# Memory chunks moved into the first two units' steps, and rotation tables computed in one pass per group

## Chip, cores and metric

The kernel runs on 1 core of one Trainium2 chip. The metric is device microseconds (us) for one execution of the whole program, the median of several runs.

## What is computed

Two encoder layers (DEPTH = 2) over one sequence of 2048 frames of 1024 channels. In each layer one projection of the input feeds four groups of heads, A (banded attention with a relative bias), B (latent attention), C (sliding window with rotary positions) and M (cross-attention into 256 memory tokens). The outputs are gated, concatenated, projected and normalized. The parts that the change touches:

```python
def _rope(x, positions):
    d = x.shape[-1]
    inv_freq = ROPE_THETA ** (-jnp.arange(0, d, 2, dtype=jnp.float32) / d)
    ang = positions.astype(jnp.float32)[..., None] * inv_freq
    cos = jnp.cos(ang)[:, :, None, :]
    sin = jnp.sin(ang)[:, :, None, :]
    x1, x2 = jnp.split(x.astype(jnp.float32), 2, axis=-1)
    return jnp.concatenate([x1 * cos - x2 * sin, x2 * cos + x1 * sin], axis=-1)

def _memory_attention(q, mem, w_mem_kv):
    kv = (mem @ w_mem_kv).reshape(b, MEM_LEN, 2, MEM_HEADS, HEAD_DIM)
    k, v = kv[:, :, 0], kv[:, :, 1]
    sc = jnp.einsum('bqhd,bmhd->bhqm', qh, k).astype(jnp.float32) * (HEAD_DIM ** -0.5)
    p = jax.nn.softmax(sc, axis=-1)
    ...
```

Group C rotates heads of 64 channels (32 frequencies, "group 0" of the tables), group B rotary parts of 32 channels (16 frequencies, "group 1").

## The kernel before

**Tiling.** The sequence is cut into four blocks of 512 frames (BT = 512, `b` = 0 to 3). A projection (`project`, L353) computes one chunk of 128 output channels for one block: eight steps over the 1024 input channels, each of three matmuls, since input and weights are kept as a high and a low part (hi x hi, hi x lo, lo x hi). A chunk's weights (512 KB) are loaded into one of two buffers `raws` (`wload`, L323) and split by ScalarE (high part) and GpSimd (low part; the first eight chunks half by VectorE) into one of two buffers `W` (`wsplit`, L328). The order of all chunks is the list `wsrc`, written out at L311 to L320 from `ORDER`: memory's eight chunks come first, then 23 per block.

**Stages.** At the start, `mem_kv` (L1193) loads memory and splits it, computes the first rotation tables, loads block 0 of x, and projects memory's chunks, first those of layer 1 (written to DRAM, read back by `load_mem`, L1230) and then those of layer 0. Between their steps it splits x. Then, for each layer, phase 1 runs six units per block: C, M and A for the first half of the heads (`p` = 0), then C, M and A for the second half. Phase 2 runs the latent attention, eight units B per layer. Phase 3 (`phase3`, L1325) is the output projection and the norm.

**Order of work.** A unit gives steps ("fill": projections, maxima, with a cost each) and banks (score and value matmuls). `drive` (L1096) runs the first unit's fill by itself and spreads each later unit's fill over the banks of the unit before it. A clock of modelled time (`Clock`, L94) puts off small pieces (`later`, `after`). Below that the framework's scheduler reorders instructions of one engine when their operands are ready, and each engine then runs its own list in order. All DMA issues here stand on SP's queue.

**Rotation tables.** `trig(b, gs)` (L279) computes cosine and signed sine of one block for a group: positions are broadcast to 128 partitions, each partition has its frequency, and the table of 128 rows x 512 holds every frequency four or eight times. It goes to DRAM (`cos`, `sin`). Before a unit that rotates, both are loaded into `cts` with one DMA each: in unit C (L731, L732), for the latents (L827, L828) and in unit B (L968, L969). The tables of group 0 of block 0 are computed in `mem_kv`, those of group 1 of block 0 at the head of unit M's fill, and those of block `b + 1`, both groups, near the head of the sixth unit's fill of block `b`, in layer 0 alone (near L1454). `rope` (L707) multiplies a projection by both tables, moves rows by four DMAs (`us<-u`) and adds.

**Other names.** `max_row` (L482) transposes the row maxima and writes them by DMA (`Y<-mr`, 4 rows of 128) into the query rows; scores wait for them. In unit B the rotated query rows go to their place by DMA (`Y<-xh`, `Y<-xl`, L1035 and L1036), which the maxima (`mx`) wait for. `Y` is one large buffer that the phases share by regions.

Of the kernel before, what the change touches and what calls it, by code (L numbers as in the profile page):

```python
# [11 lines left out]
F32 = mybir.dt.float32  # L12
# [137 lines left out]
def hybrid(ctx, tc, x, mem, positions, w_in, rel_bias, q_norm, w_uq, kv_norm, w_ukv,  # L150
# [117 lines left out]
    cosT, sinT, memkv = {}, {}, {}  # L268
# [10 lines left out]
    def trig(b, gs=(0, 1)):  # L279
        pi = tmp("pi", I32)  # L280
        dma(pi, rowcast(positions, b * BT, BT))
        pf = tmp("pf")
        nc.vector.tensor_copy(pf, pi)
        for g in gs:
            ang, kk = tmp("ang"), tmp("kk")
            nc.vector.tensor_scalar(ang, pf, rc[:, g:g + 1], None, op0=OP.mult)
            nc.vector.tensor_scalar(kk, ang, float(np.float32(1.0 / TWO_PI)), ROUND, op0=OP.mult, op1=OP.add)
            nc.vector.tensor_scalar(kk, kk, -ROUND, None, op0=OP.add)
            for pc in (PC1, PC2, PC3):
                stt(ang, kk, -pc, ang, op0=OP.mult, op1=OP.add)  # L290
            nc.vector.tensor_scalar(ang, ang, 3.1415925, -3.1415925, op0=OP.min, op1=OP.max)
            nc.vector.tensor_scalar(kk, ang, -1.0, None, op0=OP.mult)
            tt(kk, kk, ang, op=OP.max)
            nc.vector.tensor_scalar(kk, kk, -1.0, float(np.float32(math.pi / 2)), op0=OP.mult, op1=OP.add)
            act(ang, ang, AF.Sin)
            act(kk, kk, AF.Sin)
            nc.vector.tensor_scalar(ang, ang, rc[:, 2 + g:3 + g], None, op0=OP.mult)
            cosT[g, b] = dram.tile([128, BT], F32, name=f"cos{g}{b}")
            sinT[g, b] = dram.tile([128, BT], F32, name=f"sin{g}{b}")
            dma(cosT[g, b], kk)  # L300
            dma(sinT[g, b], ang)
# [26 lines left out]
    def wsplit(i):  # L328
        if i < wstate["limit"] and wstate["split"] == i:
# [108 lines left out]
    def put_v(p, vt, t0, n):  # L438
# [3 lines left out]
        def tr():  # L442
# [6 lines left out]
            ck.tick(0.107 * n)  # L449
        after(vf, 0.1, tr)  # L450
# [274 lines left out]
    def unit_c(l, b, p, D):  # L725
# [4 lines left out]
        def tabl():  # L730
            dma(cts[0], cosT[0, b])  # L731
            dma(cts[1], sinT[0, b])  # L732
# [44 lines left out]
        if p == 0:  # L777
# [41 lines left out]
    def latent(l, b, k, p, D):  # L819
# [6 lines left out]
        if k == 0:  # L826
            dma(cts[0], cosT[1, b])  # L827
            dma(cts[1], sinT[1, b])  # L828
# [71 lines left out]
    def unit_m(l, b, p, D):  # L900
# [30 lines left out]
        fill = project((l, b, 14 + 2 * p), qdone)  # L931
        pg = project((l, b, 15 + 2 * p), gdone)
# [16 lines left out]
    def unit_b(l, b, p, D):  # L949
# [13 lines left out]
        def loads():  # L963
# [4 lines left out]
            dma(cts[0], cosT[1, b])  # L968
            dma(cts[1], sinT[1, b])  # L969
# [223 lines left out]
    def mem_kv(kq):  # L1193
        ms = [region(4096 + 2048 * i, 2048).rearrange("p (k c) -> p k c", k=8) for i in range(2)]
        f, st = load_cols([mem[128 * k:128 * k + 128, :] for k in range(8)], 256, xs=ms, ahead=4)
# [12 lines left out]
        wload(3)  # L1208
        early()
        kq()  # L1210
        for ll in range(L - 1, -1, -1):
            for p in range(2):
                def kd(pk, p=p):
                    for i in range(2):
                        split_k(pk[64 * i:64 * i + 64, :256], *Km[2 * p + i])
                run_fill(mix(project(("mem", ll, p), kd, 256, xs=ms), xst[:2]))
                xst = xst[2:]
                run_fill(mix(project(("mem", ll, 2 + p), lambda pv, p=p: put_v(pv, Vm[p], 0, 2), 256, xs=ms), xst[:2]))
                xst = xst[2:]
            if ll:  # L1220
                ck.drain()
                for h in range(4):
                    for i, n in ((0, 128), (1, 64)):
                        memkv[ll, h, i] = dram.tile([n, 256], F32R, name=f"mk{ll}_{h}_{i}")
                        dma(f32(memkv[ll, h, i]), f32(Km[h][i])[0:n])
                for p in range(2):
                    memkv[ll, p] = dram.tile([128, 2, 6, 64], F32R, name=f"mv{ll}_{p}")
                    dma(f32(memkv[ll, p]), f32(Vm[p]))
# [189 lines left out]
    for l in range(L):  # L1418
# [10 lines left out]
        if l == 0:  # L1429
            mem_kv(kq)  # L1430
            ck.drain()
# [3 lines left out]
        units = []  # L1435
        for b in range(NB):
# [82 lines left out]
```

## Time and profile before

| | |
|---|---|
| median of 3 runs | 2660.25 us (2650.18 to 2664.6) |
| profiled execution, its own time | 2660.33 us |
| its span, first to last instruction | 2658.5 us |
| mean clock granted to TensorE | 0.984 of full |
| HBM traffic | 247.43 MB read, 68.02 MB written |

The profile is of one execution. Its page lists each engine's busy time; "L350" is line 350 of the kernel, which for helpers is the helper's line, so groups are told apart by their tiles (`out<-in`). PE is TensorE, DVE is VectorE, ACT is ScalarE, POOL is GpSimd, SP the queue that issues the DMAs. A bracket behind an instruction gives the engine's idle time before it and what released it. Times in a timeline are from the start of the span.

### The profile page before, as it was taken

The page shows a single profiled execution, that of the slowest core. Times are in us where ns is not written, and L with a number is a line of the kernel's source. Part 1 is how long each engine was busy: PE and PEld are TensorE (multiplying, and loading weights), DVE is VectorE, ACT ScalarE, POOL GpSimd, SP SyncE. Part 2 cuts the span into 40 slices and gives each one's busy share as a digit, 9 for nine tenths or more (in the row PEclk, how much of TensorE's full clock was granted, in tenths as well). Part 3 has the DMA queues.
Part 4 walks back from the last instruction along what each step waited for, and adds up shares of the span by engine and source line. Part 5 has one row for each costly group of instructions (what it writes and reads, how often), then busy time and mean ns, then how long its engine had stood idle before and what let it go on. Part 6 is the DMA issues. An engine that isn't in the chain of part 4 may idle for free. (4 is left out here: it accounts for less than half of the span.)

```text
span 2658.5 us, 36518 instructions
## 1 busy us (share of the span) xinstructions
PE 2517.0 (95%) x12312; PEld 2072.1 (78%) x12312; DVE 1864.5 (70%) x3309; ACT 1258.8 (47%) x2251; POOL 1071.2 (40%) x835
## 2 busy tenths in 40 slices
PE   7999999999999899989999999999999999999998
PEld 6777877877888777768877778788788777777786
DVE  4667767658666877878766566567567577588786
ACT  4544455545544566650025444454454555666200
POOL 3343434343443344353343434434434433435343
PEclk9999999999999999999999999999999999999999
DMA  6555345345345423244445443443443453232432
GB/s 208 159 159 168 107 140 158 110 132 166 106 129 169 150 78 98 71 152 145 140 136 160 150 145 127 126 138 118 143 139 115 144 168 104 68 114 78 150 124 87
DMA packets 176443, 350.90 MB, mean 132 GB/s; under 512 B 25689, under 2 KB 48945, under 8 KB 176257
## 3 DMA queue, kind: packets, MB, share of 16 engines
q1 hardware_dynamic: 176256, 348.58, 41.9%
q8 instruction: 98, 1.61, 0.3%
q14 instruction: 89, 0.72, 0.1%
HBM read 247.43 MB, written 68.02 MB: 119 GB/s over the span
## 5 line engine op out<-in xcount | busy, mean ns | idle before, releaser
L182 POOL TENSOR_TENSOR wlo<-raw,whi 128x1024 fp32r<-128x1024 f32 (+1 forms) x192 | 459.5, 2393 | 660.5 <-ACT whi L170 622.9
L350 PE MATMUL pp<-xh,whi 128*128 128x512 f32 x1472 | 591.8, 402 | 7.0 <-DVE Y L174 4.4
L350 PE MATMUL pp<-xl,whi 128*128 128x512 f32 x1472 | 583.4, 396 | 4.6 <-DVE xl L174 4.5
L350 PE MATMUL pp<-xh,wlo 128*128 128x512 f32 x1472 | 580.1, 394 | 0.0
L170 ACT ACTIVATE ph<-sc 128x512 fp32r<-128x512 f32 (+2 forms) x560 | 324.1, 579 | 359.5 <-PE sc L350 350.5
L350 PE MATMUL sc<-Y 96*128 96x512 f32 (+16 forms) x1840 | 454.8, 350 | 11.8 <-DMA Y<-mr 5.8
L174 DVE TENSOR_TENSOR pl<-p,ph 128x512 fp32r<-128x512 f32 (+2 forms) x389 | 319.6, 823 | 186.9 <-ACT p L170 182.2
L350 PE MATMUL pv<-ph,Y 128*128 128x512 f32 (+3 forms) x1520 | 396.7, 341 | 9.3 <-DVE e L178 5.4
L350 PEld LDWEIGHTS sc<-Y 96*128 96x128 f32 (+6 forms) x1840 | 315.9, 193 | 56.0 <-DMA Y<-mr 5.7
L170 ACT ACTIVATE whi<-raw 128x1024 fp32r<-128x1024 f32 x192 | 203.6, 1060 | 325.2 <-PE pp L350 119.2
L182 POOL TENSOR_TENSOR pl<-p,ph 128x512 fp32r<-128x512 f32 (+1 forms) x171 | 221.1, 1293 | 329.0 <-ACT p L170 243.5
L350 PEld LDWEIGHTS pp<-xh,whi 128*128 128x128 f32 x1472 | 279.6, 190 | 63.1 <-issue 5.1
L350 PEld LDWEIGHTS pp<-xh,wlo 128*128 128x128 f32 x1472 | 278.7, 189 | 59.2
L170 ACT ACTIVATE p<-sc 128x512 f32<-128x512 f32 (+2 forms) x560 | 322.4, 576 | 0.8 <-DVE pl L174 0.4
L350 PEld LDWEIGHTS pp<-xl,whi 128*128 128x128 f32 x1472 | 279.9, 190 | 49.8 <-DVE xl L174 6.7
L350 PEld LDWEIGHTS pv<-ph,Y 128*128 128x128 f32 x1520 | 271.3, 191 | 50.1 <-issue 5.9
L350 PE MATMUL pv<-pl,Y 128*128 128x512 f32 (+3 forms) x760 | 265.0, 349 | 34.3 <-DVE pl L174 22.4
L350 PE MATMUL mx<-Y 128*128 128x256 f32 (+6 forms) x800 | 249.6, 339 | 23.7 <-DVE Y L178 10.9
L495 DVE CUSTOM_DVE_ANT_0 mx<-mx,bts 128x128 f32<-128x128 f32 (+3 forms) x352 | 171.9, 495 | 73.3 <-PE mx L350 66.7
L350 PEld LDWEIGHTS mx<-Y 128*128 128x128 f32 (+1 forms) x800 | 148.4, 191 | 77.8 <-DVE Y L178 17.7
L182 POOL TENSOR_TENSOR g<-g,e 128x128 f32<-128x128 f32 x192 | 116.6, 616 | 206.3 <-DVE e L190 191.6
L350 PEld LDWEIGHTS pv<-pl,Y 128*128 128x128 f32 x760 | 145.4, 191 | 65.6 <-DVE pl L174 33.5
(235 smaller groups left out, 3594.4 us busy)
## 6 DMA issues: line engine op xcount, KB each, us to landing
raw<-in_w_in_dram SPq DMA_DIRECT2D x184, 512.0 KB
Y<-Y SPq DMA_DIRECT2D x144, 128.0 KB
gr<-gT SPq DMA_DIRECT2D x64, 256.0 KB
gT<-g SPq DMA_DIRECT2D x48, 256.0 KB
cts<-sin SPq DMA_DIRECT2D x40, 256.0 KB
cts<-cos SPq DMA_DIRECT2D x40, 256.0 KB
xt<-in_xT_dram SPq DMA_DIRECT2D x32, 256.0 KB
raw<-in_w_out_dram SPq DMA_DIRECT2D x16, 512.0 KB
```

What stands on the lines that cost most here:

```text
L170: return nc.scalar.activation(out, a, fn, **kw)
L174: return nc.vector.tensor_tensor(out, a, b, **kw)
L182: return nc.gpsimd.tensor_tensor(out, a, b, **kw)
L350: mm(o, lhs, rhs, start=start, stop=stop)
L495: nc.vector.tensor_tensor_reduce(m, m, table, op0=OP.add, op1=OP.max, scale=1.0, scalar=floor, accum_out=acc)
```

## The change

Rotation tables: `trig` now makes one table per group for all four blocks. Partitions 32b to 32b + 31 take block b's positions (`trig_pos`, four DMAs of 32 rows), so a pass over 128 x 512 holds 32 rows of frequencies for each block. Its thirteen parts are a list of steps. The table in DRAM has 384 rows: cosine, and sine with both signs, the second sign made by one more VectorE instruction. `tload` builds `cts` from it: the cosine with one DMA that repeats 32 rows four times, the sine with two (group 0) or four DMAs (group 1) that each take rows of both signs. Group 0's pass is mixed with the splits of x at the start, group 1's with the second unit's steps.

Memory: `mem_kv` is replaced by `start`, which loads x rather than memory, and `mem_steps`, which gives the steps of one memory chunk. Layer 0's first two chunks stand behind the four projections of the first unit (now in the order V, gate, K, Q), the other two at the head of the second unit's fill, and layer 1's four behind the second unit's query projection. Layer 1's keys and values are made in regions of `Y` that belong to group A's buffers, stored to DRAM as before, and A's setup waits, in the modelled clock, until they are. The list of weight chunks follows (`FIRST`), and the first fourteen chunks rather than eight have their low part split between VectorE and GpSimd.

```diff
+    def trig_pos():
+
         pi = tmp("pi", I32)
-        dma(pi, rowcast(positions, b * BT, BT))
-        pf = tmp("pf")
-        nc.vector.tensor_copy(pf, pi)
...
+        for b in range(NB):
+            dma(pi[32 * b:32 * b + 32], bass.AP(tensor=positions.tensor, offset=positions.offset + b * BT,
+                                                ap=[[0, 32], [1, BT]]))
+        return pi
...
+        def start():
+            st["a"], st["k"] = tmp("ang"), tmp("kk")
+            nc.vector.tensor_copy(st["k"], pi)
+
+        def sine():
+            act(st["a"], st["a"], AF.Sin)
+            act(st["k"], st["k"], AF.Sin)
+            t = trigt[g] = dram.tile([3 * 128, BT], F32, name=f"trig{g}")
+            dma(t[0:128], st["k"])
+            dma(t[128 * (1 + g):128 * (2 + g)], st["a"])
+
+        def neg():
+            st["n"] = tmp("nsin")
+            nc.vector.tensor_scalar(st["n"], st["a"], -1.0, None, op0=OP.mult)
+            dma(trigt[g][128 * (2 - g):128 * (3 - g)], st["n"])
+        return [start,
...
+                sine, neg]
+
+    def tload(g, b):
+        t = trigt[g][32 * b:32 * b + 1, 0:1]
+        n = 32 >> g
+        dma(cts[0], bass.AP(tensor=t.tensor, offset=t.offset, ap=[[0, 4], [BT, 32], [1, BT]]))
+        for i in range(2 + 2 * g):
+            r = slice(2 * n * i, 2 * n * i + 2 * n)
+            dma(cts[1][r], bass.AP(tensor=t.tensor, offset=t.offset + 128 * BT,
+                                   ap=[[(128 + g * n) * BT, 2], [BT, n], [1, BT]]))
...
-    for ll in range(L - 1, -1, -1):
-        for i in (0, 2, 1, 3):
-            wadd(("mem", ll, i), w_mem[ll, i])
     ORDER = ([8, 10, 9, 11], [14, 15], [0, 2, 1, 3], [12, 18, 19, 20, 13], [16, 17], [4, 6, 21, 5, 22, 7])
+    FIRST = [9, 11, 8, 10, (0, 0), (0, 2), (0, 1), (0, 3), 14] + [
+        (ll, i) for ll in range(1, L) for i in (0, 2, 1, 3)] + [15]
     for l in range(L):
         for b in range(NB):
-            for u in ORDER:
-                for c in u:
+            for c in FIRST + sum(ORDER[2:], []) if l == b == 0 else sum(ORDER, []):
+                if isinstance(c, tuple):
+                    wadd(("mem",) + c, w_mem[c])
+                else:
                     wadd((l, b, c), w_in[l, c])
     wend = [wpos[l, 0, 8] for l in range(1, L)] + [len(wsrc)]
     wstate = dict(loaded=0, split=0, limit=wend[0])
...
-            if i < 4 * L:
+            if i < len(FIRST):
...
-            dma(cts[0], cosT[0, b])
-            dma(cts[1], sinT[0, b])
+            tload(0, b)
...
+        if p == l == b == 0:
+            fill = project((l, b, 9), lambda pp: put_v(pp, Vc, 1, 4)) + pg + fill
+            fill += project((l, b, 8), lambda pp: rope(pp, kdone)) + pq
+            fill += mem_steps(0, 0) + mem_steps(0, 2)
+            late = maxes(0) + maxes(1)
+        elif p == 0:
...
+        if p == l == b == 0:
+            fill = mem_steps(0, 1) + mem_steps(0, 3) + fill
+            for ll in range(1, L):
+                for i in (0, 2, 1, 3):
+                    fill += mem_steps(ll, i)
...
-            dma(cts[0], cosT[1, b])
-            dma(cts[1], sinT[1, b])
+            tload(1, b)
...
+    def mem_steps(ll, i):
+
+        p = i % 2
+        if ll == 0:
+            ks, vs = Km, Vm
+        else:
+            ks = [(region(10240 + 512 * h, 256), region(10240 + 512 * h + 256, 256)) for h in range(4)]
+            vs = [vview(12288 + 768 * q, 2) for q in range(2)]
+
+        def kd(pk):
+            for z in range(2):
+                h = 2 * p + z
+                split_k(pk[64 * z:64 * z + 64, :256], *ks[h])
...
+        def keep():
+            if ll:
+                memkv[ll, p] = dram.tile([128, 2, 6, 64], F32R, name=f"mv{ll}_{p}")
+                dma(f32(memkv[ll, p]), f32(vs[p]))
+                kept.append(p)
+
+        def vd(pv):
+            if ll:
+                nc.gpsimd.memset(f32(vs[p])[:, :, 1, :], 1.0)
+                nc.gpsimd.memset(f32(vs[p])[:, :, 4, :], 0.0)
+            put_v(pv, vs[p], 0, 2, keep)
+        kept = []
...
+        if ll and i > 1:
+            mem_done.append(lambda: len(kept) > 0)
+        return r
...
+    def start(kq):
+        dma(rc, rope_c)
+        pos = trig_pos()
         wload(0)
+        f, st = load_cols(x_cols(0), BT, ahead=5, tmp=gate_tmp)
         f()
-        dma(rc, rope_c)
-        trig(0, (0,))
         wload(1)
-        run_fill(st)
         wsplit(0)
-        wsplit(1)
-        f, xst = load_cols(x_cols(0), BT, ahead=5,
-                           tmp=lambda name: sb.tile([128, BT], F32, name=name, tag="gate", bufs=6))
-        f()
-        wload(2)
-        wload(3)
+        for t in mix([z for _, z in st], trig(0, pos)):
+            t()
         early()
         kq()
...
-                us[2] = ([(0.0, lambda: (ka(), bias_tables(l, D)))] + us[2][0], us[2][1])
+                us[2] = ([(0.0, lambda: ([ck.until(m) for m in mem_done], ka(), bias_tables(l, D)))] + us[2][0], us[2][1])
             if l == 0 and b == 0:
-                us[1][0].insert(0, (0.0, lambda: trig(0, (1,))))
-            if l == 0 and b + 1 < NB:
-                us[5][0].insert(2, (0.0, lambda b=b: trig(b + 1)))
+                us[1] = (mix(us[1][0], [(0.0, lambda: tg.extend(trig(1, trig_pos())))]
+                             + [(0.0, lambda: tg.pop(0)())] * 13),) + us[1][1:]
```

## Rows read from the trace of the kernel before

**Rows 1.** Page, engines: busy us, share of the span, instructions

```profile
PE 2517.0 (95%) x12312; PEld 2072.1 (78%) x12312; DVE 1864.5 (70%) x3309; ACT 1258.8 (47%) x2251; POOL 1071.2 (40%) x835
```

**Rows 2.** Stretches: length, busy us (instructions) by engine, PEclk granted, DMA share, GB/s

```profile
0.00:52.60 52.60, 33.23 (x198) 30.67 (x198) 27.72 (x52) 27.29 (x47) 22.13 (x39) 0.94 0.74 223
52.60:92.57 39.97, 39.18 (x176) 31.33 (x177) 20.59 (x36) 17.05 (x27) 14.40 (x6) 0.96 0.50 154
```

**Rows 3.** Timeline, TensorE: start us, duration us, instruction, matmuls merged [idle before]

```profile
30.77 0.40 PE L350 MATMUL pp<-Y,whi 128*128 128x256 f32 x2
...
31.13 0.40 PE L350 MATMUL pp<-Y,whi 128*128 128x256 f32 x2
...
52.80 0.48 PE L350 MATMUL pp<-xh,whi 128*128 128x512 f32 x1
...
60.17 0.39 PE L350 MATMUL pp<-xl,whi 128*128 128x512 f32 x1
60.40 0.39 PE L350 MATMUL pp<-xh,wlo 128*128 128x512 f32 x1
```

**Rows 4.** Waits, TensorE, 0 to 60 us: us in total, times, longest us

```profile
PE pp L350 <- ACT Y L170: 8.4, 3, 5.8
```

**Rows 5.** Stretches of layer 0 and layer 1, first to fourth latent table load

```profile
147.50:758.10 610.60, 582.67 (x2920) 483.49 (x2919) 427.94 (x785) 307.91 (x520) 243.17 (x166) 0.98 0.44 137
1450.00:2049.10 599.10, 585.11 (x3017) 485.04 (x3016) 381.78 (x716) 292.51 (x502) 240.44 (x166) 1.00 0.42 133
```

**Rows 6.** The same stretch of layer 1, input transposes (tile px) alone

```profile
1450.00:2049.10 599.10, 14.06 (x96) 11.54 (x96) 15.40 (x24) 13.79 (x24) 1.00 0.42 133
```

**Rows 7.** Timeline, TensorE, after tables were computed in layer 0

```profile
216.16 1.19 PE L350 MATMUL pv<-ph,Y 128*128 128x512 f32 x2 [5.36 <-DVE e L178]
217.15 0.63 PE L350 MATMUL pp<-xh,whi 128*128 128x512 f32 x1
...
396.99 0.51 PE L350 MATMUL mx<-Y 128*128 128x256 f32 x2 [3.29 <-DVE e L178]
```

**Rows 8.** Tile ang: count, duration ns min/median/max, first and last start us

```profile
L178 DVE SCALAR_TENSOR_TENSOR ang<-kk,ang x24: 677/679/693, 17.3 to 620.4; 128x512 f32<-128x512 f32 x24
L286 DVE TENSOR_SCALAR ang<-pf,rc x8: 382/486/2612, 15.3 to 602.0; 128x512 f32<-128x512 f32 x8
...
L291 DVE TENSOR_SCALAR ang<-ang x8: 411/416/2623, 20.3 to 621.6; 128x512 f32<-128x512 f32 x8
```

**Rows 9.** Timeline, ScalarE: first and last of six weight splits in the start

```profile
31.61 1.06 ACT L170 ACTIVATE whi<-raw 128x1024 fp32r<-128x1024 f32 x1 [1.68 <-DMA raw<-in_w_mem_kv_dram]
...
51.09 1.06 ACT L170 ACTIVATE whi<-raw 128x1024 fp32r<-128x1024 f32 x1 [0.80 <-DMA raw<-in_w_in_dram]
```

**Rows 10.** Timeline, VectorE: last splits of x; first query's rope and last split

```profile
29.44 1.42 DVE L174 TENSOR_TENSOR xl<-xt,xh 128x512 fp32r<-128x512 f32 x2 [0.42 <-ACT xh L170]
...
65.58 0.69 DVE L174 TENSOR_TENSOR u<-pp,cts 128x512 f32<-128x512 f32 x1 [1.27 <-PE pp L350]
...
75.10 0.68 DVE L178 SCALAR_TENSOR_TENSOR Y<-us,Y 64x512 fp32r<-64x512 f32 x1
```

**Rows 11.** Page, DMA issues: count, KB each (cosine alike)

```profile
cts<-sin SPq DMA_DIRECT2D x40, 256.0 KB
```

**Rows 12.** DMA in 979.5 to 982 us (only `Y<-mr`), and to 984 us

```profile
DMA packets 8, 0.00 MB, mean 1 GB/s; under 512 B 4, under 2 KB 8, under 8 KB 8
...
q1 hardware_dynamic: 144, 0.25, 15.0%
```

**Rows 13.** Timeline, SP's queue, phase 2 of layer 0

```profile
1030.12 0.43 SPq L969 DMA_DIRECT2D cts<-sin  x1
1032.15 1.20 SPq L1035 DMA_DIRECT2D Y<-xh  x2
```

**Rows 14.** Timeline, TensorE: first maxima that read those query rows

```profile
1034.55 0.50 PE L350 MATMUL mx<-Y 96*128 96x512 f32 x2
```

More of the change, by code (lines that the diff above doesn't have):

```diff
@@ L266, in mla_kv @@
         return [4096 + 1024 * (b - 1), 4096 + 3072 + 1024 * (b - 1), 4096 + 6144 + 1536 * (b - 1)]
-    cosT, sinT, memkv = {}, {}, {}
+    trigt, memkv = {}, {}
     h_src = [x[0, t * 128:(t + 1) * 128, :] for t in range(S // 128)]
@@ L277, in setup_rows @@
             dma(f32(rowt)[:, c0:c1], f32(rr)[0:32, 0:c1 - c0])
-    def trig(b, gs=(0, 1)):
+    def trig_pos():
         pi = tmp("pi", I32)
-        dma(pi, rowcast(positions, b * BT, BT))
-        pf = tmp("pf")
-        nc.vector.tensor_copy(pf, pi)
[L284 to L301, printed above, removed]
@@ new lines, in trig_pos, with trig, sc, red @@
+        for b in range(NB):
+            dma(pi[32 * b:32 * b + 32], bass.AP(tensor=positions.tensor, offset=positions.offset + b * BT,
+                                                ap=[[0, 32], [1, BT]]))
+        return pi
+    def trig(g, pi):
+        st = {}
+        def sc(o, i, *c, **k):
+            return lambda: nc.vector.tensor_scalar(st[o], st[i], *c, **k)
+        def red(pc):
+            return lambda: stt(st["a"], st["k"], -pc, st["a"], op0=OP.mult, op1=OP.add)
+        def start():
[12 more added lines that the diff above has]
+        return [start,
+                sc("a", "k", rc[:, g:g + 1], None, op0=OP.mult),
+                sc("k", "a", float(np.float32(1.0 / TWO_PI)), ROUND, op0=OP.mult, op1=OP.add),
+                sc("k", "k", -ROUND, None, op0=OP.add)] + [red(pc) for pc in (PC1, PC2, PC3)] + [
+                sc("a", "a", 3.1415925, -3.1415925, op0=OP.min, op1=OP.max),
+                sc("k", "a", -1.0, None, op0=OP.mult),
+                lambda: tt(st["k"], st["k"], st["a"], op=OP.max),
+                sc("k", "k", -1.0, float(np.float32(math.pi / 2)), op0=OP.mult, op1=OP.add),
+                sine, neg]
@@ L436, in split_k, with put_v @@
         dma(f32(k1)[64:128], f32(k1)[0:64])
-    def put_v(p, vt, t0, n):
+    def put_v(p, vt, t0, n, then=lambda: None):
         vf = tmp("vf")
@@ L449, in tr @@
             ck.tick(0.107 * n)
+            then()
         after(vf, 0.1, tr)
@@ L967, in loads @@
                 dma(f32(lat[1])[64 * z:64 * z + 64, 0], f32(D["lathl"][1, b])[:, BT * z:BT * z + BT])
-            dma(cts[0], cosT[1, b])
-            dma(cts[1], sinT[1, b])
+            tload(1, b)
             for i in range(2):
@@ L1191, in bias_tables, with gate_tmp @@
             dma(D["bt"][h], bt)
-    def mem_kv(kq):
-        ms = [region(4096 + 2048 * i, 2048).rearrange("p (k c) -> p k c", k=8) for i in range(2)]
-        f, st = load_cols([mem[128 * k:128 * k + 128, :] for k in range(8)], 256, xs=ms, ahead=4)
+    ms = [region(4096 + 2048 * i, 2048).rearrange("p (k c) -> p k c", k=8) for i in range(2)]
+    def gate_tmp(name):
+        return sb.tile([128, BT], F32, name=name, tag="gate", bufs=6)
+    def mem_steps(ll, i):
[10 more added lines that the diff above has]
+                if ll:
+                    for j, n in ((0, 128), (1, 64)):
+                        memkv[ll, h, j] = dram.tile([n, 256], F32R, name=f"mk{ll}_{h}_{j}")
+                        dma(f32(memkv[ll, h, j]), f32(ks[h][j])[0:n])
+        def keep():
[4 more added lines that the diff above has]
+        def vd(pv):
+            if ll:
+                nc.gpsimd.memset(f32(vs[p])[:, :, 1, :], 1.0)
+                nc.gpsimd.memset(f32(vs[p])[:, :, 4, :], 0.0)
+            put_v(pv, vs[p], 0, 2, keep)
+        kept = []
+        r = project(("mem", ll, i), vd if i > 1 else kd, 256, xs=ms)
+        if (ll, i) == (0, 0):
+            f, st = load_cols([mem[128 * k:128 * k + 128, :] for k in range(8)], 256, xs=ms, ahead=4, tmp=gate_tmp)
+            r = [(0.0, f)] + st + r
+        if ll and i > 1:
+            mem_done.append(lambda: len(kept) > 0)
+        return r
@@ L1209, in mem_kv @@
         early()
         kq()
[L1211 to L1228, printed above, removed]
@@ L1429, in hybrid @@
         if l == 0:
-            mem_kv(kq)
-            ck.drain()
+            start(kq)
         else:
@@ L1435, in hybrid @@
         units = []
+        tg = []
         for b in range(NB):
```

2 lines of the change are left out of this document (1 added, 1 removed).

## The prediction

> **What bounds the kernel now.** The page's table of engines comes first: TensorE is busy 95% of the span [rows 1]. What can be won is time in which TensorE stands or runs at the lower of its clocks, and the table of stretches says where that is. Up to 52.6 us TensorE is busy 33.2 us; from there to 92.57 us it is busy 39.2 of 40 [rows 2]. In the first stretch it projects the eight memory chunks. At full clock three of their matmuls start every 0.36 us (30.77 to 31.13), so a chunk of 24 takes 2.9 us and eight take 23 us; the first matmul on x starts at 52.80 us [rows 3]. So 52.6 - 23.0 = 29.6 us of the start are lost. The list of waits says to what, first of all to splits by ScalarE of what has just landed, the longest 5.8 us [rows 4].
>
> The second place is found by comparing layers. From the first latent's load of its rotation tables to the fourth block's, layer 0 takes 610.6 us and layer 1 599.1 us, with the clock granted 0.98 and 1.00 of full [rows 5]. Layer 1 has 14.1 us more on TensorE there, the transposes of its input [rows 6], and yet is faster. What only layer 0 has is the rotation tables of the next block, computed three times in that stretch on VectorE, in the sixth unit's steps. There TensorE's longest waits are 5.36 and 3.29 us, both on VectorE, and after the first a 512-column matmul lasts 0.63 us [rows 7] where the profile has 0.39 elsewhere [rows 3].
>
> **The tables in one pass per group.** The old code runs eight passes (four blocks, two frequency groups), each of eleven VectorE instructions: four of 0.68 us, two of 0.49, five of 0.42, some 5.8 us [rows 8]. The new code runs two, since 32 rows of frequencies by four blocks fill the 128 partitions. Six passes go, 6 x 5.8 = 35 us of VectorE, and with them two changes of ScalarE's table per block. One negation per pass (0.42 us) comes in, and eight position loads take the place of five: nothing, since both stand in the start or beside projections. What of the 35 us lies on the path is told by the layers: 610.6 - 599.1 = 11.5 us if the transposes cost layer 1 nothing, 11.5 + 14.1 = 25.6 us if they cost it all they take. I take **-20 us**, nearer the upper end because TensorE is 98% busy in layer 1 [rows 5], so added work there lengthens it; the bounds are -11.5 and -25.6. Late next, in the same places, are the splits of x for the next block, which layer 1 has too.
>
> **The start.** Rope constants and four position loads now precede the first weight chunk on SP's queue, at about 0.44 us an issue (0.43 for the one at 1030.12 [rows 13]), so the first matmul moves from 5.8 us to some 8. The first projection then needs all of x, 2 MB, and two weight chunks, 1 MB. Loads moved 223 GB/s over the old start [rows 2]: 3.1 MB with positions take 14 us after the first issue. VectorE needs 8 x 0.7 us for the splits of x (two take 1.42 [rows 10]) and 6.7 us for the pass mixed in, 12 us from the first landing, so 20 us, less where the scheduler lets the pass start on the positions before x is there. I take 18 us for the end of the first projection, whose own work is 24 x 0.23 = 5.4 us [rows 3]: 12.6 us lost. Of the memory chunks' work nothing is saved; they move to where x can be projected beside them. Weights pass through two buffers: in the old start six weight chunks were split (51.09 - 31.61) / 5 = 3.9 us apart [rows 9], 1.0 us more than their work. Each new run of four has its first two loaded under 5.4 us projections, so 4 x 1.0 = 4 us stay. The query's rope needs 10 us from its projection to the last split (65.58 to 75.78 [rows 10]); two memory chunks cover all but 1 to 2 us. Restarts at the lower clock take 1.5 us. Lost after: 12.6 + 4 + 1.5 + 1.5 = 19.6, against 29.6: **-10 us**. The bounds are -1, if all eight chunks pay 1 us and VectorE's burst of ropes, splits and half subtractions holds TensorE another 5; and -17, if x is there by 14 us and scores fill the gaps. Splitting six more weight chunks between VectorE and GpSimd costs 0.7 us of VectorE each beside 5.4 us of projection: nothing, and 4 us if the cover is gone. Layer 1's memory keys and values pass through group A's buffers; A's mask rows, memsets and splits wait for their stores, and GpSimd's weight subtractions stand behind such a memset. Unit A's steps come behind both units, the stores before the end of the second: nothing, or up to 3 us if a memset is put too early; this is inside the bounds.
>
> **The table loads.** Forty loads of `cts`, each two transfers of 256 KB [rows 11], become 16 of three transfers and 24 of five, 88 more issues of 0.4 us on SP; their sources lead with a dimension of 4 (cosine) or 2 (sine). No load gets shorter, so there is no gain. The low end is 0: the issues lie in a queue that mostly waits. For the high end the nearest row is a transfer of 4 rows: it left 8 packets, 4 under 512 bytes and 4 of data, as if 4 engines had moved it [rows 12]. In a stretch of 4.5 us 0.25 MB, 122 packets of 2 KB, took 15% of 16 engines [rows 12]: 0.15 x 16 x 4.5 / 122 = 0.09 us each. Were a table to run on as many engines as its leading dimension, the busiest would carry 32 cosine and 64 sine rows, 8.6 us instead of 16 rows and 1.4 us, and what is issued behind it would be late. In phase 2 (latent attention) one unit's sine table is issued at 1030.12 us, the query rows that the maxima need at 1032.15 [rows 13], and the maxima start at 1034.55 [rows 14]: the high end there is 1030.1 + 8.6 - 1034.6 = 4.1 us. Fourteen loads stand like this, 57 us. But such a wait needs the sine load ahead of the query rows and no slack behind, which I expect in a third of them. I take **+10 us**.
>
> The sum: the profiled execution took 2660.33 us for a span of 2658.5, which is the median of the runs, 2660.25. 2660.3 - 20 - 10 + 10 = **2640 us**.
>
> **Rivals.** *The gains cancel.* Weight loads hold the start (a gain of 3) and the table loads cost 20: 2660 - 20 - 3 + 20 = 2657 us. For it speaks the 3.9 us between splits [rows 9]; against it that x's projections cover loads.
>
> *Narrow table loads decide, slower.* Two engines carry all sine rows, and transfers behind them (query rows, row maxima, weights) end late on exactly those. At 50 us in phase 2 and 10 in the 24 loads of phase 1 the sum is 2630 + 60 = 2690 us. It decides as soon as the forty loads expose more than 43 / 40 = 1.1 us each (30 us of gains and 13 more). For it speaks that four rows left four completions [rows 12]; against it that TensorE mostly has other attention work ready. The Trainium skill's page "DMA: Bandwidth & Descriptors" (Rules for kernel authors) states the same as a rule: a leading zero-stride broadcast of c copies confines a transfer to at most c engines. By that rule the time would be 2690 us, or near 2650 where the delays are hidden; [rows 12] agree with it for a small transfer, and no run so far shows it for a large one.
>
> *The start isn't shortened.* If x had been held by something other than the order of the steps, only the tables gain: 2660 - 20 + 10 = 2650 us. The last split of x began at 29.44 us [rows 10] and its first matmul at 52.80, so this is weak.
>
> **How the numbers follow.** A measurement of this kernel tells 0.5%, 13 us, from no change. The forecast's case (2618 to 2647) has 0.42; the cancelling case with the third rival (2647 to 2673) 0.35; the slower one 0.23. The range, 2616 to 2688, begins at the forecast's bounds (2660 - 25.6 - 17 = 2618) and reaches to the slower case's own value; the forecast's own range is 2618 to 2647.
>
> **What would show it.** Right: the first matmul on x at about 8 us and TensorE dense from 18 us on; layer 0's stretch shorter by some 20 us, without waits of over 2 us on VectorE in the sixth unit; layer 1's unchanged. The narrow rival shows as waits of TensorE on query rows or row maxima in phase 2, alike in both layers. I am wrong on the start if weight loads release most waits up to 80 us, and wrong on the tables if the layers' stretches don't draw together.

## The result, and the profile after

The changed kernel takes 2690.64 us (median of 4 runs, 2689.29 to 2691.44) against 2658.3 us for the kernel before (4 runs, 2650.18 to 2664.6): a ratio of 1.0122, with a 95% interval of 1.0097 to 1.0147. It is 32 us slower; the forecast was 20 us faster, and the time lies 2.6 us above the range. It is the time that the slower rival gave.

The page's table of engines, to be laid beside [rows 1]:

```profile
PE 2528.2 (94%) x12312; PEld 2078.0 (77%) x12312; DVE 1828.2 (68%) x3246; ACT 1243.6 (46%) x2233; POOL 1064.1 (40%) x839
```

VectorE has lost 36 us of work, close to the 35 that the prediction counted, and TensorE does the same 12312 matmuls. So the question is where TensorE stands. I cut both spans at the same instructions: at the first and the fourth block's rotation of the latent key in each layer (`ta<-pp,cts` on VectorE), at the first `xr<-xr,cts` of phase 3, and where layer 1 starts. The stretches are then the start, phase 1 from there on, phase 2, phase 3 of layer 0, layer 1 up to its first latent, and layer 1's phases 1, 2 and 3. TensorE alone; columns: length, busy us (instructions), granted clock, DMA share, GB/s. Before:

```profile
0.00:159.50 159.50, 133.57 (x661) 0.95 0.59 179
159.50:773.60 614.10, 586.12 (x2939) 0.98 0.44 137
773.60:1197.80 424.20, 395.35 (x1888) 0.98 0.39 120
1197.80:1368.00 170.20, 168.53 (x759) 1.00 0.40 134
1368.00:1462.00 94.00, 91.13 (x443) 1.00 0.54 168
1462.00:2064.70 602.70, 588.53 (x3035) 1.00 0.42 133
2064.70:2488.40 423.70, 393.73 (x1888) 0.98 0.38 117
2488.40:2658.50 170.10, 160.02 (x706) 0.98 0.34 112
```

After:

```profile
0.00:162.30 162.30, 134.01 (x661) 0.94 0.58 177
162.30:759.10 596.80, 579.31 (x2939) 1.00 0.44 135
759.10:1199.40 440.30, 398.07 (x1888) 0.97 0.38 116
1199.40:1369.60 170.20, 168.53 (x759) 1.00 0.40 132
1369.60:1476.60 107.00, 95.97 (x442) 0.95 0.49 146
1476.60:2080.80 604.20, 589.46 (x3035) 1.00 0.43 133
2080.80:2519.40 438.60, 402.87 (x1888) 0.96 0.37 113
2519.40:2689.30 169.90, 159.99 (x706) 0.98 0.33 112
```

Line by line the differences are +2.8, -17.3, +16.1, 0, +13.0, +1.5, +14.9 and -0.2, together the 30.8 us between the spans. The gain is there, in layer 0's phase 1. The loss is in both phases 2, alike, and in the first steps of layer 1, where no table is computed and no memory chunk projected: all that the change altered there is how the tables are loaded. Part of the loss is not idle time but slower work: in layer 1's phase 2 TensorE idles 35.7 us instead of 30.0, and the same 1888 matmuls are busy 9.1 us longer at a granted clock of 0.96 in place of 0.98.

The clearest place is the start of layer 1. From the timeline, SP's queue issues the tables of its first unit and then stores two tiles of phase 3's output:

```profile
1370.54 1.13 SPq L328 DMA_DIRECT2D cts<-trig  x2
1371.77 0.54 SPq L325 DMA_DIRECT2D cts<-trig  x1
1372.40 0.96 SPq L1455 DMA_DIRECT2D h<-xr  x2
```

What follows, on VectorE (first two lines) and on TensorE:

```profile
1379.94 0.69 DVE L174 TENSOR_TENSOR u<-pp,cts 128x512 f32<-128x512 f32 x1 [7.72 <-DMA cts<-trig]
1382.97 0.69 DVE L174 TENSOR_TENSOR t<-pp,cts 128x512 f32<-128x512 f32 x1 [2.34 <-DMA cts<-trig]
...
1390.95 1.12 PE L474 MATMUL pvt<-identr,vf 128*128 128x128 f32 x4 [5.97 <-ACT vf L170]
1391.71 0.78 PE L379 MATMUL pp<-xh,whi 128*128 128x512 f32 x1
...
1406.43 1.27 PE L379 MATMUL sc<-Y 73*128 73x256 f32 x6 [2.24 <-DMA raw<-in_w_in_dram]
```

The same rope in the kernel before:

```profile
1371.85 0.69 DVE L174 TENSOR_TENSOR u<-pp,cts 128x512 f32<-128x512 f32 x1 [1.18 <-DMA cts<-sin]
```

The key's rope waits 7.7 us for the sine and 2.3 more for the cosine. ScalarE, whose next work belongs to that rope, comes to the copy `vf` late, and TensorE stands 6 us and then runs a matmul in 0.78 us. In the kernel before, the rope began after a wait of 1.2 us, and TensorE did not stand there.

The trace's semaphore events tell why. Each transfer leaves its arrivals on a semaphore; here are those of four transfers of the change and one of the kernel before, in us, "|" between those that come early and those that come late. I call a transfer narrow when its source leads with 2 or 4, and wide when it leads with 16 or more.

```
change, sine piece issued 1370.54:    1371.52 | 1375.83 1376.04
change, sine piece issued 1371.15:    1372.08 | 1379.58 1379.82
change, cosine issued 1371.77:        1372.72 | 1378.69 1378.90 1382.11 1382.95
change, h<-xr issued 1372.40:         1374.40 ... 1374.56 (12) | 1378.97 1379.15 1382.76 1383.40
before, h<-xr issued 1370.15:         1372.81 ... 1373.05 (16)
```

Sixteen arrivals is what a wide transfer leaves. A sine piece leaves one early arrival and two, a cosine one early and four, just as `Y<-mr` with its four rows does (the transfer of [rows 12]). The second piece ends 3.75 us after the first: by this reading the same two engines carry 32 rows more, beside rows of the cosine and of the stores. And the store `h<-xr`, which is wide, has twelve arrivals after 2.2 us and the last four 6.6 to 11.0 us after its issue: it is not done before the loaded engines are. The Trainium skill's page "DMA: Bandwidth & Descriptors" (section "Why a DMA increments its semaphore by 16 and not by 1") says that a transfer from this queue runs on the largest number of engines, up to 16, that divides the leading sizes of both sides, that these are the lowest-numbered ones, and that the rest of the sixteen increments come at once. The events agree in count: two late arrivals in each of the 128 sine pieces, four in each of the 40 cosines, and sixteen in the stores `h<-xr`. Which engines they are the trace doesn't number.

In phase 2 the same is seen at the place of [rows 13, 14]. SP's queue, and TensorE's first maxima on the new query rows:

```profile
1028.62 0.55 SPq L325 DMA_DIRECT2D cts<-trig  x1
1029.26 0.62 SPq L328 DMA_DIRECT2D cts<-trig  x1
1031.18 1.21 SPq L1072 DMA_DIRECT2D Y<-xh  x2
...
1036.06 0.53 PE L379 MATMUL mx<-Y 96*128 96x512 f32 x2 [2.31 <-DMA Y<-xh]
```

The query rows' first transfer landed 1.96 us after its issue before (1032.15 to 1034.11); now it takes 4.74 (1031.18 to 1035.92), twelve of its arrivals in by 1033.42. Over all 32 such transfers the median from issue to last arrival went from 2.0 to 4.5 us, and the longest weight load (`raw`) from 7.1 to 11.0.

Yet these waits are the smaller part of what the phases 2 lost. The list of TensorE's waits in layer 0's phase 2 has

```profile
PE sc L379 <- DMA Y<-mr: 5.6, 3, 4.2
PE mx L379 <- DMA Y<-xh: 5.5, 3, 2.3
```

(us in total, times, longest us). With layer 1's 6.0 and 1.1 that is 18.2 us on row maxima and query rows, where the kernel before has 5.7: 12.5 of the 31.0 us. Another 11.8 are the same matmuls at the lower clock (2.7 in layer 0, 9.1 in layer 1), and the rest is spread over other waits.

The queue itself is held up too. Its issues take eight semaphores in turn (222 issues on each in the change), and each of the 1768 issues that take one again comes after the transfer that had it has landed. So while a table piece is late, SP's queue can stand and issue nothing. Its waits on table pieces, over the whole run (us in total, times, longest us), are headed by those of the next piece:

```profile
SPq L328 <- DMA cts<-trig: 33.2, 17, 4.1
```

With the smaller groups they come to 50.1 us, where the kernel before has none on its tables. How much of that TensorE felt isn't shown.

### The profile page after: what moved, and what is told of

Its sections match the earlier page's. It is cut to its first block, busy times and chain, and to the rows that moved or that the text cites. A ratio compares the mean times of both kernels' runs of the same rounds, so it can differ in the third digit from the quotient of the medians.

```text
span 2689.3 us, 36492 instructions
## 1 busy us (share of the span) xinstructions
PE 2528.2 (94%) x12312; PEld 2078.0 (77%) x12312; DVE 1828.2 (68%) x3246; ACT 1243.6 (46%) x2233; POOL 1064.1 (40%) x839
## 5 line engine op out<-in xcount | busy, mean ns | idle before, releaser
L182 POOL TENSOR_TENSOR wlo<-raw,whi 128x1024 fp32r<-128x1024 f32 (+1 forms) x192 | 453.4, 2361 | 679.5 <-ACT whi L170 634.9
L379 PE MATMUL sc<-Y 96*128 96x512 f32 (+16 forms) x1840 | 461.2, 354 | 24.3 <-DMA Y<-mr 15.5
L379 PEld LDWEIGHTS sc<-Y 96*128 96x128 f32 (+6 forms) x1840 | 319.9, 195 | 70.2 <-DMA Y<-mr 12.5
L379 PEld LDWEIGHTS mx<-Y 128*128 128x128 f32 (+1 forms) x800 | 149.6, 193 | 91.3 <-DVE Y L178 18.4
```

The source lines that it names most:

```text
L182: return nc.gpsimd.tensor_tensor(out, a, b, **kw)
L379: mm(o, lhs, rhs, start=start, stop=stop)
```

## The experiments

**Theory N**: the narrow table loads cost the time, and without them the change gains. **Rivals**: another part of the change lengthens those stretches (O); the 88 more issues on SP's queue do (I); the common planes, not the number of engines, do (P). All ratios are against the kernel before, run beside it on the same chip. The code cuts below are shortened; `AP` stands for a hand-made access pattern with its list of [step, count].

| run | median us | ratio, 95% interval |
|---|---|---|
| narrow_alone (cosine only) | 2674.92 | 1.0068 (1.0047 to 1.0089) |
| issues_alone | 2665.47 | 1.0032 (1.0018 to 1.0046) |
| sine_narrow | 2687.29 | 1.0107 (1.0091 to 1.0123) |
| both_narrow | 2715.58 | 1.0218 (1.0201 to 1.0234) |
| change_wide | 2623.74 | 0.9879 (0.9852 to 0.9907) |
| change_pieces | 2633.20 | 0.9903 (0.9889 to 0.9918) |
| tables_wide | 2637.86 | 0.9933 (0.9912 to 0.9954) |
| memory_alone | 2655.83 | 0.9985 (0.9971 to 0.9999) |
| lead_four | 2699.17 | 1.0139 (1.0123 to 1.0156) |
| lead_two | 2761.98 | 1.0381 (1.0359 to 1.0402) |
| spare_wide | 2659.39 | 0.9998 (0.9987 to 1.0009) |
| spare_narrow | 2788.63 | 1.0483 (1.0468 to 1.0497) |
| wide_behind | 2657.97 | 0.9999 (0.9989 to 1.0010) |
| two_behind | 2729.29 | 1.0275 (1.0261 to 1.0289) |

The stretches of the profiled executions, cut as above (us; phase 3 of layer 0 and the start of layer 1 in one):

| run | start | 0: phase 1 | 0: phase 2 | to layer 1's latent | 1: phase 1 | 1: phase 2 | rest |
|---|---|---|---|---|---|---|---|
| before | 159.5 | 614.1 | 424.2 | 264.2 | 602.7 | 423.7 | 170.1 |
| after | 162.3 | 596.8 | 440.3 | 277.2 | 604.2 | 438.6 | 169.9 |
| change_wide | 149.6 | 589.3 | 422.6 | 264.0 | 601.7 | 422.2 | 169.9 |
| tables_wide | 166.1 | 589.3 | 423.4 | 264.2 | 601.9 | 420.8 | 169.9 |
| memory_alone | 152.5 | 617.1 | 420.7 | 264.2 | 603.0 | 426.2 | 170.0 |
| both_narrow | 164.6 | 618.2 | 436.7 | 276.2 | 608.3 | 438.8 | 170.0 |

### The narrow loads by themselves, and their number

The kernel before got only the change's way of loading.

```diff
-            dma(cts[0], cosT[g, b]); dma(cts[1], sinT[g, b])
+            dma(cts[0], AP(cosT, [[0, 4], [BT, 32], [1, BT]]))
+            for i in range(2 + 2 * g):   # n = 32 >> g
+                dma(cts[1][2*n*i:2*n*i + 2*n], AP(sinT, row 2*n*i, [[n * BT, 2], [BT, n], [1, BT]]))
```

> The kernel before, in which only the forty loads of the rotation tables are issued as the change issues them: cosine as one transfer whose source leads with 4, sine as two or four transfers whose sources lead with 2, from the old per-block tables, which hold the same values. Theory N (few engines carry a narrow load, and what is issued behind it is late): the stretches that grew under the change and hold no other part of it, phase 2 of layer 0 (+16.1 us), the start of layer 1 (+13.0) and phase 2 of layer 1 (+14.9), grow alike, so 2658 + 44 = 2702 us, 2690 to 2712. Theory O (something else of the change, such as layer 1's memory tiles or the one pass, lengthens these stretches): 2655 to 2668 us.

It has 1.0068, 18 us, which is under theory N's range and above theory O's. The events say why: all 128 sine transfers have sixteen arrivals. In the old table the two halves of a piece lie one behind the other, so they are one block of rows, and only the cosine was narrow (40 loads with one early arrival and four).

The same number of issues, all wide:

```diff
+            dma(cts[0], cosT[g, b])
+            for i in range(2 + 2 * g):
+                dma(cts[1][2*n*i:2*n*i + 2*n], sinT[g, b][2*n*i:2*n*i + 2*n])
```

> The kernel before with as many transfers per table load as the change has (three for a load of group 0, five for one of group 1), each of whole rows of the old table, so that every source leads with 128, 64 or 32. Theory N (few engines): nothing to see, 2655 to 2668 us. Theory I (the 88 more issues on SP's queue delay what stands behind them): as the loads alone, 2690 us or more; at 0.4 to 0.6 us for each of 88 issues at most 53 us.

1.0032, 8 us: inside theory N's range, but the interval lies above 1, so issues aren't free, some 0.1 us each. They are not the loss.

Then the sine with halves that lie apart, with the cosine narrow and without:

```diff
-                ... AP(sinT, row 2*n*i, [[n * BT, 2], [BT, n], [1, BT]])
+                ... AP(sinT, row 0, [[3 * n * BT, 2], [BT, n], [1, BT]])   # same values
```

> The kernel before with its table loads issued as the change issues them, and now the two halves of each sine source lie apart, as in the change (in the earlier run they lay one behind the other, and the trace shows sixteen arrivals for each of those sine transfers, so only the cosine was narrow there). The same values are read. Theory N: the narrow loads cost here what they cost in the change, 2690.6 - 2623.7 = 67 us, less what is due to the tables' own place: 2705 to 2730 us. Theory P (the price comes from the change's planes, twelve of whose loads read the same rows of one tensor, and not from the number of engines): 2670 to 2682 us, as with the cosine alone.

> The kernel before with the cosine in one wide transfer and only the sine in two or four transfers that lead with 2. Theory N: 64 of the 96 rows on the busiest engine are the sine's; cosine alone with all issues had +17.4, the issues alone +7.9, so the cosine has some 9.5 us and the sine the rest of 67: 2658 + 67 - 9.5 = 2715, 2695 to 2722 us. Theory P: 2662 to 2670 us, as the issues alone.

Both narrow: 1.0218, 58 us by the ratio, as theory N had it; theory P falls. Its stretches grow where the change's do (phases 2 by 12.5 and 15.1, the start of layer 1 by 12.0). The sine alone has 1.0107, 28 us, under theory N's range and above theory P's: the two don't add up. Cosine 18 and sine 28, each with 8 of issues in it, make 38 together, and together they cost 58.

### The change with wide loads, and its two parts

The tables keep their one pass per group. From its planes each block's rows are copied out, 32 at a time, to full tables of 128 rows, beside the steps of the first unit M and of the last unit A of blocks 0 to 2; block 0's first table is written from SBUF.

```diff
+    def copies(g, b, c, s):        # four steps, spread over a unit's
+        ...
+            dma(cosT[g, b][32 * q:32 * q + 32], c)
+            dma(sinT[g, b][32 * q:32 * q + 32], s[q % 2])
 ...
     def tload(g, b):
-        dma(cts[0], bass.AP(..., ap=[[0, 4], [BT, 32], [1, BT]]))
-        for i in range(2 + 2 * g): ...
+        dma(cts[0], cosT[g, b])
+        dma(cts[1], sinT[g, b])
```

> The changed kernel, whose tables, still computed in one pass per group, are copied out to a full table of 128 rows per block and group, and loaded by two transfers that lead with 128. Theory N: the three stretches return to their old lengths and layer 0's phase 1 keeps its gain of 17 us, so 2690.6 - 44 = 2647 us, 2636 to 2652; the start shortens too if its ropes waited for narrow tables. Theory O: 2680 us or more.

0.9879: 32 us faster than before and 67 us faster than the change (by the ratios 65). It beats both kernels, and by more than expected, for the start and layer 0's phase 1 had carried narrow loads as well. Some of its stretches (TensorE, columns as above):

```profile
0.00:149.60 149.60, 128.62 (x661) 0.97 0.63 196
149.60:738.90 589.30, 578.28 (x2939) 1.00 0.45 143
738.90:1161.50 422.60, 395.32 (x1888) 0.97 0.38 121
...
2027.20:2449.40 422.20, 394.81 (x1888) 0.98 0.37 117
```

The phases 2 are back at their old lengths, and the query rows take 2.0 us again. Against it the change loses 12.7 us in the start, 7.5 in layer 0's phase 1, 17.7, 13.2, 2.5 and 16.4 behind: 70 us between the spans.

The same planes can be loaded wide without a copy, by more transfers:

```diff
+        for i in range(4):
+            dma(cts[0][32 * i:32 * i + 32], t[32 * b:32 * b + 32])
+        for i in range(4 + 4 * g):
+            o = 128 * (1 + i % 2) + 32 * b + g * n * (i % 2)
+            dma(cts[1][n * i:n * i + n], t[o:o + n])
```

> The changed kernel with its planes as they are, and each table loaded by transfers of one contiguous block of rows: four of 32 for the cosine, four of 32 or eight of 16 for the sine; 416 transfers in place of 168, none of which leads with fewer than 16. Theory N: 2690.6 - 67 = 2624, and 248 more issues at 7.9 / 88 = 0.09 us each: 2646, 2630 to 2655 us. Theory P (planes): 2690 us or more. If SP's queue becomes the limit with 8 to 12 issues of 0.5 us ahead of the query rows: 2660 to 2690 us.

0.9903, inside theory N's range: 416 transfers of 16 or 32 rows do far better than 168 narrow ones, and a little worse than 80 wide ones. Here the planes, the passes and the places of the loads are the change's own, and only the leading sizes and the number of transfers differ: the start is down to 146.6 us, the phases 2 to 426.0 and 427.0, the stretch to layer 1's latent to 266.5.

The parts: `tables_wide` is the kernel before with the pass and the copies and its own start; `memory_alone` is the change with the old `trig` and wide loads.

> The kernel before, memory chunks first as there, with the tables in one pass per group, copied out to full tables and loaded by two wide transfers: the tables' part alone without its narrow loads. The pass is worth the 17.3 us by which layer 0's phase 1 shortened, or the 20 of the prediction: 2638 to 2645 us. If the copies' 64 transfers or the mixing of the pass into the steps gives that back: 2652 us or more. Against the run with both parts it tells what the memory chunks' move is worth: the prediction has -10 us, the stretch up to the first latent +2.8 us with narrow loads in it.

> The changed kernel with the old tables (eight passes, one for each block and group, full tables, wide loads): the memory chunks' move alone. The prediction's step has -10 us, bounds -1 to -17; the difference of the two wide runs has 2623.7 - 2637.9 = -14.1. 2640 to 2651 us if the two parts add up; near 2658 if the move pays only where the pass is short.

The tables have 0.9933, 18 us. In layer 0's phase 1 they gain 24.8 us; the old start gives 6.6 back. Eleven table writes stand there on SP's queue from 26.78 to 31.85 us, ahead of memory's last four loads, and the first matmul on x is at 66.6 us, 52.8 before. The move alone has 0.9985, 4 us, its start 7.0 us shorter; with the tables' pass in both kernels it brings 14 us (2637.86 to 2623.74). The parts don't add up: 18 and 4 us alone, 32 together, and `memory_alone` lies above the 2640 to 2651 us that adding up would have given, nearer to the 2658 of a move that pays only where the pass is short. In the stretches both together shorten the start by 9.9 us and layer 0's phase 1 by 24.8; alone the tables have +6.6 and -24.8 there, the move -7.0 and +3.0. So beside the move the pass no longer lengthens the start; the 3.0 us are not explained.

### What a narrow transfer does to others

Only group 1's 24 loads, two transfers each as before, with a leading zero stride:

```diff
+        for d, t in zip(cts, (cosT[g, b], sinT[g, b])):
+            dma(d, AP(t, [[0, K], [BT, 128 // K], [1, BT]]) if g else t)   # K = 4, 2
```

> The kernel before; the 24 loads of group 1's tables alone (eight of latents, sixteen in phase 2) have sources that lead with a zero stride of 4, one transfer for each table as before, the other sixteen loads stay wide: no more issues than before, 32 + 32 rows on the busiest engine in place of 8 + 8. Theory N with a price that grows with the rows on the busiest engine: the two phases 2, +12.5 and +15.1 us with 96 rows, take up to two thirds of that, so 2660 + 5 to 18 = 2665 to 2678 us. If only a lead of 2 hurts: 2655 to 2664 us.

> The same 24 loads with sources that lead with a zero stride of 2: 64 + 64 rows on each of two engines. Theory N: more than the 28 us of both_narrow's phases 2 (96 rows on the busiest), 2688 to 2710 us, and at least twice the growth of lead_four. If the price does not go with the rows on the busiest engine but with the number of narrow transfers: the same as lead_four.

1.0139 and 1.0381, 37 and 101 us: both above their ranges, and lead_two 2.7 times lead_four. My measure of size, the rows on the busiest engine, is wrong: the phases 2 grow by 24.7 and 18.6 us with the 64 rows of lead_four, by 12.5 and 15.1 with the 96 of both_narrow (and by 54.9 and 37.7 in lead_two). In these three runs the growth goes with how long the query rows take: medians of 2.0 us before, 4.6 in both_narrow, 5.8 with a lead of 4 and 8.9 with a lead of 2. It isn't the whole price: sine_narrow's query rows take 2.2 us (median), hardly longer than before, and its phases 2 still grow by 7.3 and 6.0. In both_narrow and sine_narrow the pieces of the sine go out in several issues, with query rows between; in lead_four and lead_two both tables go out back to back ahead of them.

A transfer that nothing reads was to tell whether the lateness is the table's own:

```diff
         dma(cts[0], cosT[g, b]); dma(cts[1], sinT[g, b])
+        dma(spare[-1], AP(sinT, [[0, 2], [BT, 64], [1, BT]]))   # spare_wide: sinT[g, b]
```

> The kernel before, its forty table loads wide as there, each followed by one more transfer of the sine table's 256 KB into a spare tensor that nothing reads, from a source that leads with a zero stride of 2: 64 rows on each of two engines, as the change's sine has. Theory B (what is issued behind a narrow transfer is late, whatever it carries): as the narrow sine without its issues, 27 - 8 = 19, and forty issues at 0.09 = 4: 2683, 2673 to 2695 us. Theory T (the ropes wait for their own late tables, and that is the price): as spare_wide, 2660 to 2670 us.

> The same forty spare transfers from a source that leads with 128: forty more issues and 10 MB more traffic, no engine loaded more than another. All theories: 2660 to 2670 us; it is the base for spare_narrow. If the traffic as such costs, spare_narrow has it too.

The wide ones cost nothing (0.9998); the narrow ones 127 us (1.0483), though no instruction reads them. That is 94 us above theory B's range. The framework's scheduler issued ten of them before layer 0's phase 1 and thirty in it, ten close together each time, so the loss stands there (725.5 us in place of 618.0 with wide ones, and 181.2 in place of 156.8 in the start), and its size isn't that of one spare behind each load. The waits of TensorE and of ScalarE in that stretch (columns: us in total, times, longest us) show whom it hit:

```profile
PE pp L359 <- ACT xh L170: 80.5, 3, 31.5
...
ACT xh L170 <- DMA xt<-in_xT_dram: 91.0, 6, 35.8
ACT whi L170 <- DMA raw<-in_w_in_dram: 31.7, 4, 14.3
```

Wide loads of x and of weights, issued behind the spares, are late: the longest load of x takes 26.1 us from issue to landing there, 6.3 with wide spares, and the longest weight load 23.3, 6.0 with wide spares. Theory T, in which only the ropes that read a late table pay, falls. But SP's queue also waits, for the semaphores that the spares hold (the three largest groups):

```profile
SPq L311 <- DMA spare<-sin: 33.5, 10, 4.4
SPq L419 <- DMA spare<-sin: 26.1, 6, 4.5
SPq L334 <- DMA spare<-sin: 24.9, 6, 4.9
```

In all it stands 126.7 us for them, and not at all for the wide ones. So the 127 us are lateness behind a narrow transfer and a queue that stands, and no run separates the two.

Last, the place in the queue: lead_two's loads, issued only behind the previous unit's query rows.

```diff
                     st["q"] = True          # query rows issued
+                    for z in range(2):
+                        nc.gpsimd.tensor_copy(cts[z][0:64, 0:1], f32(ql_)[:, 0:1])
+                    tload(1, next b)
```

> The run lead_two (2762 us, +100), in which phase 2 issues each unit's tables, narrow as there, only behind the previous unit's query rows: two copies of one column on GpSimd, from the last split of the query rows into the table tiles, make the loads wait for it. In lead_two all the waits of TensorE on query rows in the two phases 2 (31.0 and 17.4 us) ended on such rows issued behind the tables. Theory B (a narrow transfer delays what is issued behind it): those 48 us all but vanish; the low half rows, the gates and the next latents are behind the tables now and have more slack, so 2690 to 2725 us. Theory C (a narrow transfer delays whatever is on its way at the same time, wherever it was issued): 2745 us or more.

> The kernel before with the same order, its tables wide: the base for two_behind. Both theories: 2650 to 2668 us; if the order itself costs (tables now 5 us later, ropes waiting for them), 2670 us or more, and that is to be taken off two_behind.

The order by itself costs nothing (0.9999). With narrow tables it takes a quarter of the loss away: 1.0275 in place of 1.0381, 4 us above theory B's range and 16 under theory C's. TensorE's longest waits between 790 and 1200 us, in layer 0's phase 2, first in lead_two:

```profile
PE mx L356 <- DMA Y<-xh: 31.0, 5, 8.2
PE sc L356 <- DMA Y<-mr: 7.8, 3, 6.4
```

and in two_behind:

```profile
PE sc L356 <- DMA Y<-mr: 18.9, 4, 9.9
PE pv L356 <- DVE pl L174: 7.3, 8, 1.3
```

The waits on query rows are gone (17.4 us in layer 1 as well), and those on the row maxima, which now stand next behind the tables, have grown from 7.8 to 18.9 and in layer 1 from 11.9 to 22.5. So the place in the queue chooses who waits; it doesn't take the wait away.

## Why the prediction was wrong

**The tables in one pass: right.** -20 us was taken, -18 measured alone (0.9933, a start longer by 6.6 included), and the layer's stretch shortened by 24.8, within the bounds of -11.5 to -25.6. The mechanism is seen too: before, TensorE stood five times for 2.2 us or more on VectorE in that stretch, and in the change the longest such wait is 1.6. The comparison of the layers gave that, and the choice nearer the upper end was the right one. Layer 1's phase 1 is unchanged (602.7 to 601.7).

**The start: right, once the loads are wide.** -10 us was taken; the start shortened by 9.9 with wide loads, though it grew by 2.8 in the change itself. The first matmul on x stands at 8.46 us, for some 8 forecast; the last of the first projection starts at 19.39, where 18 was forecast for its end. The other terms of that sum, the 1.5 us of restarts at the lower clock among them, weren't measured one by one. By whole runs the move is worth 14 us beside the pass and 4 alone. The rival that the start isn't shortened falls, and so does the one in which the gains cancel for want of weights.

**The table loads: the step that failed.** "Such a wait needs the sine load ahead of the query rows and no slack behind, which I expect in a third of them. I take +10 us." They cost 65 to 67 us, the price of the change against change_wide, 57 against change_pieces. The step failed in three ways. It priced only fourteen loads of phase 2; those phases lost 34 us of the 57 that were the high end, but as much again (12.7 + 7.5 + 13.2 + 2.5 = 36) was lost where no cost was set, mostly at the starts of the layers, where the tables are needed at once (in layer 1's the rope itself waited 10 us for them). It counted the wait on the query rows alone, which came to no more than 6.6 us in the two phases 2, while other transfers behind a narrow one are late too, down to a store and a weight load, the clock fell with the waits, and SP's queue itself stood 50 us for table pieces. And its own chance doesn't give its number: a third of 57 is 19 us, and 10 was taken without a reason. The price of a row was right: 0.09 us was taken, and in lead_two the second of two loads of 64 rows on the same engines lands 5.45 us behind the first (median of 18 pairs), 0.085 a row. At the place of [rows 13] TensorE waited 2.3 us, where 4.1 was the high end. So a single delay was not sized too small; what was missed is where else, and how else, it counts. The low end of 0 for the issues was wrong as well: wide pieces in the same number cost 8 us.

**The slower rival** had the mechanism, and the phases 2 grew alike in both layers (+16.1 and +14.9). Its marks, waits on query rows and row maxima, are there, but they are 12.5 us of that growth. Its 2690 us is the time measured. That it meets it so closely is partly luck: its split, 50 in phase 2 and 10 in phase 1, is not what was measured. The range was said to reach to this case's own value, but it ended at 2688. I gave it 0.23 because "TensorE mostly has other attention work ready". In phase 2 that was partly so, as 34 of 57 shows; at the start of layer 1 TensorE stood 6 us. [Rows 12] already showed four data packets for four rows, and a chance of a half would have been nearer to what was read from it.

## What to carry to other kernels

Look at the leading size of each access pattern before counting a transfer's bytes: 256 KB with a leading size of 2 held up what was issued behind it for several microseconds, and at times the issuing queue itself, whether or not anyone read it. Where compute is saved by storing a table once, pay for its copies when it is written, or load it by pieces of 16 or more rows; both kept the whole gain here, or most of it. And an edit whose cost you can't see in the profile deserves a price at each place where it stands, not only where the queue looked full.

## What the runs showed of the hardware

- Two halves of a source that follow one another in memory count as one block: sixteen arrivals in narrow_alone, three (one early, two later) once they lie apart, for the same values.
- Two kinds of narrow loads cost more together than their sum: cosine 1.0068, sine 1.0107, each with the 1.0032 of the issues in it, both 1.0218.
- A transfer that nothing reads can still stop the queue that issued it, through the semaphore that a later one needs: 126.7 us of such waits behind forty narrow spares, none behind forty wide ones.
- The granted clock followed the waits: over layer 1's first steps 0.95 in place of 1.00, over the phases 2 of lead_two 0.92 and 0.94 in place of 0.98, so that a us of wait cost more than a us (in layer 1's phase 2 of the change 5.7 us more idle time came with 9.1 us more of busy time for the same matmuls).

Left open is how the 65 us divide between ropes that waited for their own tables, transfers that were late behind them, and a queue that stood; the spares show the last two without the first, but not at the change's places.
